# A hybrid attention and state-space block: the tables of W_out made earlier and kept in DRAM, and no elementwise sums on GpSimd behind the attention

## The chip, the cores and the metric

The kernel runs on one core of a Trainium2 chip. A core has TensorE (matmuls, PE in the profile; PEld is its weight load), VectorE (DVE), ScalarE (ACT), GpSimd (POOL) and SyncE (SP), which here only issues DMAs. Each engine works through its own list of instructions in order and waits at semaphores for the others; ScalarE's and GpSimd's lists can hold DMA issues too. The metric is the device time of one execution in microseconds: the median over runs.

## The reference

One layer on a sequence of 1024 tokens with 1024 features, float32. Cut to what matters:

```python
h = rms_norm(x, norm_gain)
q, k, v, z_a, u, z_s, g_a, g_s = split(h @ w_in)         # 4*512 + 2*512 + 2*1024 columns
y_a = (band_attention(q, k, v) * silu(z_a)) @ w_attn_out  # 8 heads of 64, chunks of 64, 9 chunks wide
y_s = gelu(s5_ssm(u))                                     # diagonal complex state space, 32 groups x 64 states
a, b = split(y_s @ w_glu + b_glu)
y_s = (a * sigmoid(b) * silu(z_s)) @ w_ssm_out
merged = sigmoid(g_a + bias_a) * y_a + sigmoid(g_s + bias_s) * y_s
out = rms_norm(x + merged @ w_out, final_gain)
```

The products have to keep float32 accuracy. The kernel splits each operand into a rounded part and the rest (`_hi` and `_lo`, type fp32r), and makes three matmuls of each product: hi x hi, lo x hi, hi x lo.

## The kernel before, in words

**Layout.** Features lie on the 128 partitions; a projection task makes 128 output features for all 1024 tokens, in two halves of 512 tokens, each accumulated in one of three PSUM banks (tag "mm"). A task is: load a block of weights (`w_raw`, 512 KB; `o_raw`, 256 KB, in the later stages), split it (`split_hi` on ScalarE, L100; `split_lo` on VectorE, L103), multiply (L106 to L108), evacuate each half. `Stream.run` loads and splits the weights of the next tasks while one is multiplied; w_hi, w_lo, o_hi and o_lo have two buffers each.

**Stages, in TensorE's order.** Norm and V; the projections of u, z and q, k with the state-space model beside them; the attention with q, k and the first five of eight g_a projections; the last g_a and the eight g_s projections (to 580 us: `ga_task`, `gs_task`, `sg` goes to DRAM as `sgs_dr`); the attention output (`a_task`, eight tasks, y_a times w_attn_out, evacuated by `mgd<-mm,mg`, L85); GLU (`glu_tasks`, eight, `zs<-zs,sg`); the SSM output (`so_task`, eight, `sg<-mm,sg` and `mgd<-mgd,sg`); and the final product with W_out.

**Beside the attention output** the state-space results are read back from DRAM in pieces of 512 bytes (`load_y`, tile `yr`) and split into `g_hi`, `g_lo`, the operands of GLU (`split_y_ssm`).

**The final product** uses Strassen's seven products instead of eight, on 2 x 2 blocks, for four blocks of 256 tokens. Its weight operands are seven tables for each of four row blocks j: B11, B21, B22 are blocks of W_out as they are, T1 to T4 are sums of them. Each table is a tile of hi and lo, 512 KB. `prepare_wo` loads two row blocks (`wo_raw`), lets GpSimd make the four sums (`t<-wo_raw`, `wo_raw<-wo_raw`, L85), and `keep` splits each table into its resident place `wb` (28 tiles, in places that `SPOTS` lists and that come free one after another). The loops over the attention output, GLU and SSM output call `next(tables)` to put a table's work between the tasks. The token side has its own sums: `derive` makes S1 to S4 (`s<-mgd`, on VectorE for the first token block and GpSimd for the others), `operand` splits them (`a`). `complete` adds up the squares and multiplies by the final gain (`x<-x,fg_b`, GpSimd).

**What sets the order.** The program is written task by task; a list scheduler with a model of the engines' and DMAs' times then orders the instructions of each engine by priority. Splits of weights have high priority. During the attention TensorE's order is as written. Tiles are reused as soon as their last reader is done, so a load into a used place waits for that reader, and what stands behind the load in its queue waits too. Before the change all loads of this part are issued by SyncE.

Of the kernel before, what the change touches and what calls it, by code (L numbers as in the profile page):

```python
# [44 lines left out]
def trunk_kernel(ctx: ExitStack, tc: tile.TileContext, x, x_t, ng, w_m, w_v, bias, a_re, a_im, log_dt,  # L45
# [38 lines left out]
    def tt(o, a, b, op, eng=None):  # L84
        (eng or vec).tensor_tensor(out=o, in0=a, in1=b, op=op)  # L85
# [1071 lines left out]
    def so_task(m, y):  # L1157
        sgs = []

        def load():  # L1160
            for half in range(2):
                sgs.append(half_tile())
                nc.sync.dma_start(out=sgs[half], in_=sgs_dr[m][:, cut(half)])

        loads.append(load)

        def before():

            for n in ([0, 1] if m == 0 else [m + 1] if m + 1 < KT else []):
                loads[n]()  # L1170

        def evac(half, ps):
            tt(sgs[half], ps, sgs[half], MUL)
            tt(merged(m, cut(half)), merged(m, cut(half)), sgs[half], ADD, pool if m < KT - 1 else vec)
        return o_task(w_so[m], y, evac, before, m == 0)

    zs = [None] * 4
# [1 line left out]
    def glu_tasks(m, y):  # L1179
        sgs = {}  # L1180

        def evac_b(half, ps):
            if half == 0:
                zs[m] = zp.tile([P, L], F32, tag="z", name="zs")
                nc.sync.dma_start(out=zs[m], in_=zs_dr[m])
            sgs[half] = half_tile()
            act.activation(out=sgs[half], in_=ps, func=AF.Sigmoid, bias=bg[:, 4 + m:5 + m])

        def evac_a(half, ps):
            sl = cut(half)  # L1190
            stt(sgs[half], ps, bg[:, m:m + 1], sgs[half], ADD, MUL)
            tt(zs[m][:, sl], zs[m][:, sl], sgs[half], MUL, pool if m < 3 else vec)

        return [o_task(w_glu[4 + m], y, evac_b), o_task(w_glu[m], y, evac_a)]

# [10 lines left out]
    def load_y(b):  # L1206
        yr = rows.tile([P, T8, NJ], F32, tag="yr", name="yr")
        nc.sync.dma_start(out=yr, in_=y_dr[b].rearrange("t p j -> p t j"))
        ygr.append(yr)

    gen = stream.run(ga[NGA:] + [gs_task(m) for m in range(KT)], a_all[:2])
    for _ in range(4 * KT):
        with tc.issue_after(last_turn[0]):
            next(gen)
    for b in range(2):
        load_y(b)
    for _ in gen:
        pass
    wp_cm.__exit__(None, None, None)
    h16_cm.__exit__(None, None, None)  # L1220
    wo_cm = tc.tile_pool(name="wo", reuse_waits="tile", side="right", bufs=14)
# [11 lines left out]
        yg[1].append(lo)  # L1233

    SPOTS = [(wo, "wb")] * 6 + [(qk_pools[n // 5], "blk") for n in range(10)] + [(wo, "wb")] * 8 + [(zp, "z")] * 4
    wb = {}
    raws = {}  # L1240

    def load_rows_wo(j):
        raws[j] = []
        for q in range(2):
            r = rows.tile([P, D], F32, tag="yr", name="wo_raw")
            nc.sync.dma_start(out=r, in_=w_out[(j + 4 * q) * P:(j + 4 * q + 1) * P, :])
            raws[j].append(r)

    def prepare_wo(j):

        def keep(name, src):
            p_, tag = SPOTS[len(wb)]
            t = p_.tile([P, 2, HALF], F32R, tag=tag, name="wb")
            split_hi(t[:, 0, :], src)
            split_lo(t[:, 1, :], src, t[:, 0, :])
            wb[name, j] = t

        def sum_tile():
            return rest.tile([P, HALF], F32, tag="t", name="t", bufs=1)

        b11, b12 = raws[j][0][:, cut(0)], raws[j][0][:, cut(1)]
        b21, b22 = raws[j][1][:, cut(0)], raws[j][1][:, cut(1)]
        t1 = sum_tile()
        tt(t1, b12, b11, SUB, pool)
        tt(b12, b22, b12, SUB, pool)
        keep("B11", b11)
        yield
        keep("T1", t1)
        t2 = sum_tile()
        tt(t2, b12, b11, ADD, pool)  # L1270
        yield
        keep("T3", b12)
        tt(b12, b21, t2, SUB, pool)
        yield
        keep("T2", t2)
        yield
        keep("B21", b21)
        yield
        keep("B22", b22)
        yield  # L1280
        keep("T4", b12)
        yield

    def all_wo():

        for j in range(4):
            load_rows_wo(j)
            yield
            yield
            for _ in prepare_wo(j):  # L1290
                yield

    tables = all_wo()

    for n, _ in enumerate(stream.run(a_all, glu[:2])):
        if n in (0, 1, 5, 6):
            split_y_ssm(len(yg[0]))
            if n < 2:
                load_y(n + 2)
        elif n > 6:  # L1300
            next(tables)
    for n, _ in enumerate(stream.run(glu, so_all[:2])):
        if n >= 3 and len(wb) < 16:
            next(tables)
    hs, ls = split_tiles(zs, vp, "v", "y", (3,))
    ys[0].extend(hs)
    ys[1].extend(ls)
# [13 lines left out]
        return t  # L1321

    for n, _ in enumerate(stream.run(so_all)):
        if n > 0:
            next(tables, None)
        if n == 2 * KT - 2:
            fin_op["A11"] = operand(block(0, "A11"), rows, "yr")
            s3 = rest.tile([P, HALF], F32, tag="t", name="s3", bufs=1).rearrange("p (k m) -> p k m", m=P)
            tt(s3, block(0, "A11"), block(0, "A21"), SUB, pool)
            fin_op["S3"] = operand(s3, rows, "yr")  # L1330
    assert len(wb) == 28
    rest_cm.__exit__(None, None, None)
# [24 lines left out]
    for n in range(KT // 2):  # L1357
# [5 lines left out]
            nc.sync.dma_start(out=xi[r], in_=x[tok[r], :])  # L1363
        ss = [fin.tile([P, 4], F32, tag=f"ss{r}", name="ss") for r in range(2)]
        blk = {b: block(n, b) for b in ("A11", "A12", "A21", "A22")}
        eng = vec if first else pool

        def derive(name, p, q, op):
            t = vp.tile([P, HALF], F32, tag="v", name="s")
            blk[name] = t.rearrange("p (k m) -> p k m", m=P)  # L1370
            tt(blk[name], blk[p], blk[q], op, eng)

        done = [0, 0]

        def complete(b, cs, end):

            r = b // 2
            col = slice((b % 2) * HALF + cs.start, (b % 2) * HALF + cs.stop)
            v = xi[r][:, col]
            sq = ps_v.tile([P, HALF], F32, tag="pv", name="sq")  # L1380
            act.activation(out=sq[:, :cs.stop - cs.start], in_=v, func=AF.Square, accum_out=ss[r][:, done[r]:done[r] + 1])
            if done[r] == 0:
                ts(ss[r][:, 3:4], ss[r][:, 0:1], 1.0 / D, MUL, 1e-6, ADD)
            else:
                stt(ss[r][:, 3:4], ss[r][:, done[r]:done[r] + 1], 1.0 / D, ss[r][:, 3:4], MUL, ADD)
            done[r] += 1
            cols[r].append(col)
            if not end:
                tt(v, v, fg_b[:, col], MUL, pool)
                return  # L1390
            inv = rsqrt(fin, ss[r][:, 3:4])
            for k, col in reversed(list(enumerate(cols[r]))):
                v = xi[r][:, col]
# [6 lines left out]
                (nc.scalar if k == 0 else nc.sync).dma_start(out=out[tok[r], col], in_=v)  # L1400
# [112 lines left out]
```

## Time and profile before

| | |
|---|---|
| median of three runs | 811.55 us (810.03 to 812.24) |
| the profiled execution | 809.46 us, span 807.7 us, clock 0.998 |
| TensorE, VectorE, ScalarE, GpSimd busy | 97%, 64%, 46%, 25% of the span |
| DMA | 76.22 MB, 94 GB/s in the mean |
| HBM read, written | 60.34 MB, 15.17 MB |

A row of the timeline has the start, the duration, the engine, the line, and the tile written <- the tiles read; in brackets stands how long the engine sat idle before and what ended that. A group's row has the number of instructions, their busy time and mean, and the idle time before them. TensorE's matmuls overlap: one starts every 0.23 us or so though each lasts 0.39, so lost time is read from their starts.

### The profile page before, as it was taken

What the parts mean: (1) busy time and instruction counts of PE and PEld (TensorE: products, weight loads), DVE (VectorE), ACT (ScalarE), POOL (GpSimd) and SP (SyncE); (2) the same over time, 40 slices, a digit from 0 to 9 for tenths busy, and PEclk for the clock granted to TensorE, in tenths of its full rate; (3) what the DMA queues carried; (4) which work ended last, traced back from release to release, by engine and by line L of the source; (5) the groups of instructions that cost most, each with busy time, mean ns of one, the idle gap of its engine ahead of it and who ended that gap; (6) DMA issues with size and microseconds to landing.
All of it is one profiled execution on the core that took longest, in us unless ns stands there. A gap on an engine that the chain in (4) does not pass through costs nothing. (4 is left out here: it accounts for less than half of the span.)

```text
span 807.7 us, 11038 instructions
## 1 busy us (share of the span) xinstructions
PE 786.7 (97%) x3882; PEld 650.8 (81%) x3882; DVE 515.6 (64%) x1324; ACT 371.5 (46%) x670; POOL 199.3 (25%) x220
## 2 busy tenths in 40 slices
PE   8999999999999999999999999999999999899996
PEld 6778888888887888888888888888867887788884
DVE  6899997978647788787445430111178338866684
ACT  5653455646436566666454572122253224322542
POOL 4560022020202323333122100000023223744431
PEclk9999999999999999999999999999999999999999
DMA  8703433233331011111000261231144114322332
GB/s 312 263 27 104 116 92 117 87 88 125 106 113 43 27 43 43 44 43 43 27 28 26 79 209 66 104 105 66 52 131 157 52 48 149 121 94 112 104 131 79
DMA packets 37063, 76.22 MB, mean 94 GB/s; under 512 B 5072, under 2 KB 14288, under 8 KB 37008
## 3 DMA queue, kind: packets, MB, share of 16 engines
q1 hardware_dynamic: 32512, 69.74, 25.6%
q0 software_dynamic: 1152, 2.36, 1.5%
q10 hardware_dynamic: 3344, 3.42, 1.3%
q8 instruction: 30, 0.49, 0.3%
q14 instruction: 25, 0.20, 0.1%
HBM read 60.34 MB, written 15.17 MB: 93 GB/s over the span
## 5 line engine op out<-in xcount | busy, mean ns | idle before, releaser
L106 PE MATMUL mm<-hT,w_hi 128*128 128x512 f32 x576 | 233.3, 405 | 0.0
L108 PE MATMUL mm<-hT,w_lo 128*128 128x512 f32 x576 | 226.1, 393 | 0.7 <-DVE w_lo L103 0.7
L107 PE MATMUL mm<-hT,w_hi 128*128 128x512 f32 x576 | 225.4, 391 | 0.0
L108 PEld LDWEIGHTS mm<-hT,w_lo 128*128 128x128 f32 x576 | 108.1, 188 | 24.6 <-DVE w_lo L103 1.1
L107 PEld LDWEIGHTS mm<-hT,w_hi 128*128 128x128 f32 x576 | 108.6, 189 | 16.6 <-issue 0.4
L106 PEld LDWEIGHTS mm<-hT,w_hi 128*128 128x128 f32 x576 | 108.4, 188 | 16.1 <-issue 0.2
L103 DVE TENSOR_TENSOR w_lo<-w_raw,w_hi 128x1024 fp32r<-128x1024 f32 x36 | 44.3, 1230 | 83.8 <-ACT w_hi L100 83.5
L939 POOL TENSOR_SCALAR p<-p,sm 128x640 f32<-128x640 f32 (+2 forms) x64 | 42.8, 671 | 111.3 <-DVE sm L938 80.8
L100 ACT ACTIVATE w_hi<-w_raw 128x1024 fp32r<-128x1024 f32 x36 | 38.1, 1058 | 68.8 <-PE mm L107 57.6
L937 ACT ACTIVATE p<-p,mx 128x640 f32<-128x640 f32 (+2 forms) x64 | 44.4, 694 | 33.3 <-DVE mx L89 16.5
L103 DVE TENSOR_TENSOR tl<-pt,th 128x512 fp32r<-128x512 f32 (+2 forms) x72 | 43.0, 600 | 24.5 <-ACT th L100 24.0
L100 ACT ACTIVATE th<-pt 128x512 fp32r<-128x512 f32 (+2 forms) x72 | 37.7, 523 | 44.5 <-PE pt L957 43.9
L930 DVE CUSTOM_DVE_ANT_0 p<-s,bias 128x320 f32<-128x320 f32 (+2 forms) x96 | 44.2, 485 | 17.1 <-PE s L929 16.7
L108 PE MATMUL mm<-y_hi,o_lo 128*128 128x512 f32 x128 | 50.2, 394 | 4.1 <-DVE o_lo L103 4.1
L106 PE MATMUL mm<-y_hi,o_hi 128*128 128x512 f32 x128 | 50.3, 394 | 1.9 <-ACT o_hi L100 1.1
L107 PE MATMUL mm<-y_lo,o_hi 128*128 128x512 f32 x128 | 49.8, 390 | 0.0
L85 POOL TENSOR_TENSOR t<-wo_raw 128x512 f32<-128x512 f32 x8 | 11.3, 1418 | 148.7 <-PE mm L108 129.9
L1427 PE MATMUL c<-wb,a 128*128 128x512 f32 (+1 forms) x116 | 44.8, 387 | 0.0
L1426 PE MATMUL c<-wb,a 128*128 128x512 f32 (+1 forms) x116 | 44.2, 387 | 0.5 <-DVE x L85 0.5
L1428 PE MATMUL c<-wb,a 128*128 128x512 f32 (+1 forms) x116 | 44.2, 385 | 0.0
L957 PE MATMUL pt<-ident,p 128*128 128x128 f32 x240 | 38.1, 273 | 0.0
L976 PE MATMUL pv<-tl,vt 128*128 128x256 f32 x144 | 36.2, 281 | 1.0 <-DVE tl L103 1.0
(230 smaller groups left out, 1533.4 us busy)
## 6 DMA issues: line engine op xcount, KB each, us to landing
w_raw<-in_w_m_dram SPq DMA_DIRECT2D x36, 512.0 KB, 3.5
x<-in_x_dram SPq DMA_DIRECT2D x16, 512.0 KB, 7.7
sgs_dr<-sg SPq DMA_DIRECT2D x16, 256.0 KB, 2.0
wo_raw<-in_w_out_dram SPq DMA_DIRECT2D x8, 512.0 KB, 3.5
sg<-sgs_dr SPq DMA_DIRECT2D x16, 256.0 KB, 2.9
xt<-in_x_t_dram SPq DMA_DIRECT2D x6, 512.0 KB, 9.6
bias<-in_bias_dram SPq DMA_DIRECT2D x8, 320.0 KB, 2.8
wv_raw<-in_w_v_dram SPq DMA_DIRECT2D x8, 256.0 KB, 5.6
```

Of the source, the lines that this page charges most:

```text
L100: act.activation(out=hi, in_=src, func=AF.Copy)
L103: (eng or vec).tensor_tensor(out=lo, in0=src, in1=hi.bitcast(F32), op=SUB)
L106: pe.matmul(ps, lh, rh, start=first, stop=False)
L107: pe.matmul(ps, lh, rl, start=False, stop=False)
L108: pe.matmul(ps, ll, rh, start=False, stop=last)
L930: vec.tensor_tensor_reduce(out=pr[:, c * cw:(c + 1) * cw], in0=ps, in1=bt[:, 640 - w + c * cw:640 - w + (c + 1) * cw], scale=1.0, scalar=- ...
L937: act.activation(out=pr[:, :w], in_=pr[:, :w], func=AF.Exp, bias=mx[:, 0:1], accum_out=sm)
L939: pool.tensor_scalar(out=pr[:, :w], in0=pr[:, :w], scalar1=sm, scalar2=1.0, op0=MUL, op1=MUL)
L957: last_turn[0] = pe.transpose(tp[:, n:n + P], probs[h, q][:, k * P:(k + 1) * P], ident).ins
L1426: pe.matmul(o, a[:, 0, k, :], h, start=new and k == 0, stop=False, skip_group_check=True)
L1427: pe.matmul(o, a[:, 0, k, :], l, start=False, stop=False, skip_group_check=True)
L1428: pe.matmul(o, a[:, 1, k, :], h, start=False, stop=k == 3, skip_group_check=True)
```

## The change

Four edits. (1) `make_tables` runs during the g_s projections, a step after every third matmul group: it loads the rows of W_out, makes the sums on VectorE, splits each table into one of the two free tiles of pool `blk1`, and stores it in DRAM (`wt_dr`, SyncE's queue). (2) `load_table` reads the 28 tables back into the same places as before, from ScalarE's queue, during the attention output, GLU and SSM output, in the order in which the final product uses them. (3) `load_y` of the first two blocks comes late in g_s instead of at its start, since its pool now holds `wo_raw`. (4) All sums and products that GpSimd made behind the attention are made by VectorE.

```diff
@@ so_task, glu_tasks
-            tt(merged(m, cut(half)), merged(m, cut(half)), sgs[half], ADD, pool if m < KT - 1 else vec)
+            tt(merged(m, cut(half)), merged(m, cut(half)), sgs[half], ADD)
-            tt(zs[m][:, sl], zs[m][:, sl], sgs[half], MUL, pool if m < 3 else vec)
+            tt(zs[m][:, sl], zs[m][:, sl], sgs[half], MUL)
@@ g_a, g_s
+    wt_dr = {(name, j): dr.tile([P, 2, HALF], F32, name=f"wt_{name}_{j}")
+             for name in ("B11", "B21", "B22", "T1", "T2", "T3", "T4") for j in range(4)}
+    def make_tables():
+        for j in range(4):
+            raws = []
+            for q in range(2):
+                r = rows.tile([P, D], F32, tag="yr", name="wo_raw")
+                nc.sync.dma_start(out=r, in_=w_out[(j + 4 * q) * P:(j + 4 * q + 1) * P, :])
+                raws.append(r)
+            yield
+            yield
+            def keep(name, src):
+                t = qk_pools[1].tile([P, 2, HALF], F32R, tag="blk", name="wt")
+                split_hi(t[:, 0, :], src)
+                split_lo(t[:, 1, :], src, t[:, 0, :])
+                nc.sync.dma_start(out=wt_dr[name, j], in_=t.bitcast(F32))
...
+            tt(t1, b12, b11, SUB)
+            tt(b12, b22, b12, SUB)
+            keep("T1", t1)
+            yield
+            keep("T3", b12)
...
-    for b in range(2):
-        load_y(b)
-    for _ in gen:
-        pass
+    for n, _ in enumerate(gen):
+        if n % 3 == 2:
+            next(tables, None)
+        if n in (3 * 36 + 4, 3 * 36 + 12):
+            load_y((n - 112) // 8)
@@ attention output, GLU, SSM output
-    def load_rows_wo(j):
-    def prepare_wo(j):
...
+    USE = ["B11", "T3", "B21", "T2", "T1", "B22", "T4"]
+    def load_table():
+        name, j = USE[len(wb) // 4], len(wb) % 4
+        p_, tag = SPOTS[len(wb)]
+        t = p_.tile([P, 2, HALF], F32R, tag=tag, name="wb")
+        nc.scalar.dma_start(out=t.bitcast(F32), in_=wt_dr[name, j])
+        wb[name, j] = t
     for n, _ in enumerate(stream.run(a_all, glu[:2])):
...
-        elif n > 6:
-            next(tables)
+        if n in (4, 7, 9, 11, 13, 15):
+            load_table()
     for n, _ in enumerate(stream.run(glu, so_all[:2])):
-        if n >= 3 and len(wb) < 16:
-            next(tables)
+        if n >= 2 and len(wb) < 16:
+            load_table()
     for n, _ in enumerate(stream.run(so_all)):
-        if n > 0:
-            next(tables, None)
+        if n > 1 and len(wb) < 28:
+            load_table()
@@ final product
-        eng = vec if first else pool
-            tt(blk[name], blk[p], blk[q], op, eng)
+            tt(blk[name], blk[p], blk[q], op)
-                tt(v, v, fg_b[:, col], MUL, pool)
+                tt(v, v, fg_b[:, col], MUL)
```

The scheduler puts the new work at these places. First ScalarE in the g_s projections: sg is the evacuation of a half (L1138), w_hi the split of the next weights. Before:

```order
L1138 ACTIVATE sg_5396<-mm_5371,gb_2612 128x512
L100 ACTIVATE w_hi_5461<-w_raw_5431 128x1024
L1138 ACTIVATE sg_5428<-mm_5403,gb_2612 128x512
L1138 ACTIVATE sg_5458<-mm_5433,gb_2612 128x512
L100 ACTIVATE w_hi_5523<-w_raw_5493 128x1024
```

and with the change, where wt is a table's buffer:

```order
L1138 ACTIVATE sg_5450<-mm_5417,gb_2612 128x512
L100 ACTIVATE wt_5457<-wo_raw_5348 128x512
L100 ACTIVATE wt_5471<-wo_raw_5348 128x512
L100 ACTIVATE w_hi_5540<-w_raw_5497 128x1024
L1138 ACTIVATE sg_5494<-mm_5461,gb_2612 128x512
L100 ACTIVATE wt_5515<-t_5512 128x512
L100 ACTIVATE wt_5528<-wo_raw_5484 128x512
L1138 ACTIVATE sg_5537<-mm_5499,gb_2612 128x512
L100 ACTIVATE wt_5551<-t_5532 128x512
L100 ACTIVATE wt_5565<-wo_raw_5484 128x512
L100 ACTIVATE w_hi_5623<-w_raw_5585 128x1024
```

Four table splits now stand between one w_hi and the next. Second, VectorE in the attention output, from the o_lo of the fourth task on. Before:

```order
L103 TENSOR_TENSOR o_lo_5961<-o_raw_5922,o_hi_5960 128x512
L103 TENSOR_TENSOR wb_6081<-wo_raw_6038,wb_6081 128x512
L103 TENSOR_TENSOR wb_6105<-t_6078,wb_6105 128x512
L85 TENSOR_TENSOR mgd_5872<-mm_5964,mg_4743 128x512
L103 TENSOR_TENSOR wb_6125<-wo_raw_6038,wb_6125 128x512
L85 TENSOR_TENSOR mgd_5872<-mm_5979,mg_4743 128x512
L103 TENSOR_TENSOR wb_6150<-t_6108,wb_6150 128x512
L103 TENSOR_TENSOR wb_6168<-wo_raw_6040,wb_6168 128x512
L103 TENSOR_TENSOR wb_6192<-wo_raw_6040,wb_6192 128x512
L103 TENSOR_TENSOR o_lo_6001<-o_raw_5958,o_hi_6000 128x512
```

and with the change, from the split of the last y_ssm block on:

```order
L103 TENSOR_TENSOR g_lo_6202<-yr_6100,g_hi_6201 128x1024
L85 TENSOR_TENSOR mgd_6052<-mm_6123,mg_4553 128x512
L103 TENSOR_TENSOR o_lo_6141<-o_raw_6102,o_hi_6140 128x512
L85 TENSOR_TENSOR mgd_6052<-mm_6144,mg_4743 128x512
L85 TENSOR_TENSOR mgd_6052<-mm_6161,mg_4743 128x512
L103 TENSOR_TENSOR o_lo_6183<-o_raw_6138,o_hi_6182 128x512
```

The six table splits (wb) between one o_lo and the next are gone. Third, VectorE in the SSM output. Before:

```order
L103 TENSOR_TENSOR wb_6896<-wo_raw_6740,wb_6896 128x512
L85 TENSOR_TENSOR sg_6629<-mm_6695,sg_6629 128x512
L103 TENSOR_TENSOR wb_6914<-wo_raw_6738,wb_6914 128x512
L103 TENSOR_TENSOR o_lo_6716<-o_raw_6667,o_hi_6715 128x512
L85 TENSOR_TENSOR sg_6673<-mm_6723,sg_6673 128x512
```

and with the change:

```order
L85 TENSOR_TENSOR sg_6758<-mm_6806,sg_6758 128x512
L85 TENSOR_TENSOR sg_6760<-mm_6823,sg_6760 128x512
L85 TENSOR_TENSOR mgd_6052<-mgd_6052,sg_6758 128x512
L85 TENSOR_TENSOR mgd_6052<-mgd_6052,sg_6760 128x512
L103 TENSOR_TENSOR o_lo_6843<-o_raw_6796,o_hi_6842 128x512
```

The two mgd sums that GpSimd made now stand ahead of the next o_lo, and the table splits are gone.

More of the change, by code (lines that the diff above doesn't have):

```diff
@@ L1209, in load_y, with sum_tile @@
         ygr.append(yr)
+    wt_dr = {(name, j): dr.tile([P, 2, HALF], F32, name=f"wt_{name}_{j}")
[14 more added lines that the diff above has]
+                nc.sync.dma_start(out=wt_dr[name, j], in_=t.bitcast(F32))
+            def sum_tile():
+                return rest.tile([P, HALF], F32, tag="t", name="t", bufs=1)
+            b11, b12 = raws[0][:, cut(0)], raws[0][:, cut(1)]
+            b21, b22 = raws[1][:, cut(0)], raws[1][:, cut(1)]
+            t1 = sum_tile()
+            tt(t1, b12, b11, SUB)
[3 more added lines that the diff above has]
+            keep("T3", b12)
+            t2 = sum_tile()
+            tt(t2, b12, b11, ADD)
+            yield
+            keep("T2", t2)
+            tt(b12, b21, t2, SUB)
+            yield
+            for name, src in (("T4", b12), ("B11", b11), ("B21", b21), ("B22", b22)):
+                keep(name, src)
+                yield
+    tables = make_tables()
     gen = stream.run(ga[NGA:] + [gs_task(m) for m in range(KT)], a_all[:2])
@@ L1238, in trunk_kernel @@
     SPOTS = [(wo, "wb")] * 6 + [(qk_pools[n // 5], "blk") for n in range(10)] + [(wo, "wb")] * 8 + [(zp, "z")] * 4
+    USE = ["B11", "T3", "B21", "T2", "T1", "B22", "T4"]
     wb = {}
-    raws = {}
-    def load_rows_wo(j):
[L1243 to L1247, printed above, removed]
-    def prepare_wo(j):
[L1251 to L1293, printed above, removed]
+    def load_table():
[4 more added lines that the diff above has]
+        wb[name, j] = t
     for n, _ in enumerate(stream.run(a_all, glu[:2])):
@@ L1328, in trunk_kernel @@
             s3 = rest.tile([P, HALF], F32, tag="t", name="s3", bufs=1).rearrange("p (k m) -> p k m", m=P)
-            tt(s3, block(0, "A11"), block(0, "A21"), SUB, pool)
+            tt(s3, block(0, "A11"), block(0, "A21"), SUB)
             fin_op["S3"] = operand(s3, rows, "yr")
```

## The prediction

> **What bounds the kernel now.** I read the page, then the busy time by stage, then what TensorE waited for, then the rows around those waits. TensorE is busy 97% of the span.
>
> ```profile
> PE 786.7 (97%) x3882; PEld 650.8 (81%) x3882; DVE 515.6 (64%) x1324; ACT 371.5 (46%) x670; POOL 199.3 (25%) x220
> ```
>
> Busy time is modelled, so I count the matmuls instead. In the g_s projections 24 of them run from 574.83 to 580.27 us, 0.2267 us each (two rows of TensorE's timeline; the second is the first row of the attention output):
>
> ```profile
> 574.83 0.39 PE L106 MATMUL mm<-hT,w_hi 128*128 128x512 f32 x1
> 580.27 0.39 PE L106 MATMUL mm<-y_hi,o_hi 128*128 128x512 f32 x1
> ```
>
> The windows are g_a/g_s, attention output, GLU, SSM output, final product; the first numbers are us, PE busy (count), PEld, DVE, ACT, POOL, then the granted clock, DMA share and GB/s:
>
> ```profile
> 480.00:580.00 100.00, 100.00 (x443) 82.81 (x442) 9.81 (x8) 21.90 (x29) 0.00 (x0) 1.00 0.22 77
> 580.27:629.51 49.24, 45.57 (x193) 35.41 (x192) 36.47 (x41) 21.60 (x27) 13.93 (x10) 1.00 0.40 129
> 629.51:674.31 44.80, 44.80 (x193) 35.91 (x192) 17.29 (x23) 15.74 (x25) 10.54 (x8) 1.00 0.21 60
> 674.31:721.22 46.91, 44.57 (x193) 35.68 (x192) 35.36 (x41) 11.77 (x21) 29.73 (x20) 1.00 0.39 129
> 721.22:799.91 78.69, 78.17 (x349) 63.48 (x347) 54.26 (x109) 32.44 (x72) 28.49 (x21) 1.00 0.27 101
> ```
>
> 192 matmuls need 43.5 us. The attention output takes 5.7 us more, GLU 1.3, SSM output 3.4. The final product has 336 full widths, 76.2 us, and takes 78.7 and the last 0.1: 2.6 more. So everything that can be won from 580 us on is 13.0 us, and 9.1 of it lies in two stages. There TensorE's waits are these (us in total, times, longest):
>
> ```profile
> PE mm L108 <- DVE o_lo L103: 4.1, 4, 1.5
> PE mm L106 <- ACT o_hi L100: 1.1, 1, 1.1
> PE mm L106 <- DVE mgd L85: 0.6, 1, 0.6
> PE mm L106 <- DVE sg L85: 0.2, 1, 0.2
> ```
>
> Seven waits, 6.0 us; with some 0.27 us hidden by the modelled ends at each, 7.9 of the 9.1. What made o_lo late, in rows of the timeline (start, us, engine): first VectorE in the attention output, then three engines in the SSM output:
>
> ```profile
> 604.95 1.28 DVE L103 TENSOR_TENSOR wb<-wo_raw,wb 128x512 fp32r<-128x512 f32 x2
> 606.15 0.68 DVE L103 TENSOR_TENSOR o_lo<-o_raw,o_hi 128x512 fp32r<-128x512 f32 x1
> ...
> 697.36 1.65 POOL L85 TENSOR_TENSOR mgd<-mgd,sg 128x512 f32<-128x512 f32 x1 [1.23 <-DVE sg L85]
> 697.81 1.75 DVE L103 TENSOR_TENSOR o_lo<-o_raw,o_hi 128x512 fp32r<-128x512 f32 x1
> 699.62 0.50 PE L108 MATMUL mm<-y_hi,o_lo 128*128 128x512 f32 x1 [1.48 <-DVE o_lo L103]
> ```
>
> Two causes: table splits (wb) stand ahead of o_lo on VectorE, and a split of two SBUF operands takes 1.75 us, not 0.68, while GpSimd adds. In the groups of 580 to 722 us the mean shows it, and mgd<-mm, which reads PSUM, does not have it:
>
> ```profile
> L103 DVE TENSOR_TENSOR wb<-wo_raw,wb 128x512 fp32r<-128x512 f32 x20 | 21.4, 1083 | 3.2 <-ACT wb L100 2.6
> L103 DVE TENSOR_TENSOR o_lo<-o_raw,o_hi 128x512 fp32r<-128x512 f32 x22 | 20.0, 909 | 7.3 <-ACT o_hi L100 7.3
> L85 DVE TENSOR_TENSOR mgd<-mm,mg 128x512 f32<-128x512 f32 x16 | 10.7, 681 | 4.2 <-PE mm L108 4.2
> ```
>
> **The change part by part.** *Attention and SSM output.* 28 splits (29 us of VectorE with their stretched durations) leave, and GpSimd is silent. VectorE gets 6 zs and 14 mgd sums here and the rest of these groups of GpSimd (580 to 808 us) in the final product:
>
> ```profile
> L85 POOL TENSOR_TENSOR mgd<-mgd,sg 128x512 f32<-128x512 f32 x14 | 21.4, 1540 | 7.5 <-DVE sg L85 7.5
> L85 POOL TENSOR_TENSOR x<-x,fg_b 128x512 f32<-128x512 f32 (+1 forms) x9 | 11.1, 1232 | 22.7 <-ACT sq L1381 19.3 <-DVE x L85 3.4
> L85 POOL TENSOR_TENSOR s<-mgd 128x512 f32<-128x512 f32 x7 | 10.6, 1513 | 23.0 <-DVE a L103 17.6 <-PE c L1428 5.3
> ```
>
> At 0.68 us an SSM task of 5.44 us then asks VectorE for two sg, two mgd and one o_lo: 3.4 us. So I leave 0.4 us of the SSM output's 3.4 (its scattered part): gain 3.0, bounds 2 and 3.4. In the attention output one wait stays. The fourth task starts at 580.3 + 3 x 5.44 = 596.6 and its o_lo is needed at 597.0, but it stands behind the last y_ssm split (VectorE's timeline; the last row is an issue of a DMA by ScalarE, from the final product):
>
> ```profile
> 594.24 2.03 DVE L103 TENSOR_TENSOR g_lo<-yr,g_hi 128x1024 fp32r<-128x1024 f32 x1 [0.22 <-ACT g_hi L100]
> 596.78 0.68 DVE L103 TENSOR_TENSOR o_lo<-o_raw,o_hi 128x512 fp32r<-128x512 f32 x1
> 753.49 0.39 ACTq L1400 DMA_DIRECT2D out_dram<-x  x1
> ```
>
> That is 0.4 us late at today's times. The new order puts table loads of 512 KB beside the last two loads of yr, 1.5 us each at the 355 GB/s worked out below, and two issues of 0.39 us on ScalarE ahead of this o_hi. Bounds 0.4 and 0.4 + 2 x 1.5 = 3.4; I take 1.4, nearer to today's row, because the issues run while VectorE still splits yr. With 0.4 scattered, gain 5.7 - 1.8 = 3.9. GLU had no named wait: 0.
>
> *The tables in g_s.* 28 ScalarE and 28 VectorE splits, 16 sums, 28 stores and 8 loads enter a stage where VectorE is busy 10% and ScalarE 22%: 17.6 us more on ScalarE, 30 on VectorE; the 92 us from 488 hold that. What can cost is waiting: in the new order ScalarE has four tables between one w_hi and the next, each waits for one of two buffers, and a buffer is free when its store has landed. Behind it stand sg and w_hi, and TensorE waits for those. The rows: two w_hi on ScalarE's timeline, the page's group of w_lo, a split of a table on ScalarE today, and DMA issues with KB and us to landing.
>
> ```profile
> 504.08 1.06 ACT L100 ACTIVATE w_hi<-w_raw 128x1024 fp32r<-128x1024 f32 x1 [4.52 <-PE mm L107]
> 514.97 1.06 ACT L100 ACTIVATE w_hi<-w_raw 128x1024 fp32r<-128x1024 f32 x1 [4.52 <-PE mm L107]
> ...
> L103 DVE TENSOR_TENSOR w_lo<-w_raw,w_hi 128x1024 fp32r<-128x1024 f32 x36 | 44.3, 1230 | 83.8 <-ACT w_hi L100 83.5
> ...
> 598.64 0.63 ACT L100 ACTIVATE wb<-t 128x512 fp32r<-128x512 f32 x1 [1.06 <-POOL t L85]
> ...
> w_raw<-in_w_m_dram SPq DMA_DIRECT2D x36, 512.0 KB, 3.5
> x<-in_x_dram SPq DMA_DIRECT2D x16, 512.0 KB, 7.7
> ...
> zs_dr<-zst SPq DMA_DIRECT2D x4, 512.0 KB, 2.9
> ```
>
> A w_hi is needed one task, 10.9 us, after it is made; less 1.06 and VectorE's 1.23 for w_lo, 8.6 us of slack. A table's cycle is 0.63 for the first split, 0.68 for the second, 0.39 for the issue and the landing of a 512 KB store: 2.9 in zs_dr's row, so 4.6 us, 2.3 per table with two buffers. The order spreads the 28 over 7.4 tasks of 10.9 us, 80 us, 2.9 each. With c = (1.7 + landing) / 2 the landing may grow to 4.7 us before 28 x (c - 2.9) eats the 8.6. Will it? The stage moves 14.7 MB of stores, 3.1 of w_out rows, 3.7 of w_raw, 3.9 of sg in 80 us: 318 GB/s. Three windows of today, with DMA share and GB/s at the end:
>
> ```profile
> 500.00:520.00 20.00, 20.00 (x90) 16.53 (x89) 2.45 (x2) 3.96 (x5) 0.00 (x0) 1.00 0.29 103
> 560.00:580.00 20.00, 20.00 (x90) 16.57 (x89) 0.80 (x1) 2.20 (x4) 0.00 (x0) 1.00 0.13 52
> 466.00:474.00 8.00, 8.00 (x37) 6.60 (x36) 0.63 (x1) 7.96 (x15) 1.20 (x1) 1.00 0.93 288
> ```
>
> 103 GB/s at share 0.29 is 355 GB/s for a full share, the stores of sg alone 52 / 0.13 = 400, the small pieces of yr 288 / 0.93 = 310. So the engines are 80 to 103% full. Cost: none up to 8.6 us of lag, 42 us with a landing like x's 7.7 (28 x (4.7 - 2.9) - 8.6; the run's first loads). I take 0, near the stores' own row.
>
> The Trainium skill, "HBM Reference", section Latency, speaks against that: an access takes 0.2 us on average and 2 us at high load. By it a store here would land some 1.8 us later, 4.7, just at the edge; the sum would lose 0 to 2 us (an estimate from that page). No run here shows a loaded store yet.
>
> *Final product and end.* VectorE takes over 12 derived sums and 9 products with fg_b, 8.3 + 5.8 = 14.1 us at 0.68 each: at most 54.3 + 14.1 = 68.4 of 78.7 us, 87%, less what GpSimd stretches now. TensorE has no wait there but 0.5 us at the end. Cost 0.2, bounds 0 and 14.1. At the end, GpSimd's and VectorE's timeline:
>
> ```profile
> 799.13 0.73 POOL L85 TENSOR_TENSOR x<-x,fg_b 128x256 f32<-128x256 f32 x1 [2.48 <-ACT sq L1381]
> ...
> 799.18 0.70 DVE L94 SCALAR_TENSOR_TENSOR rs_u<-rs_r,ss 128x1 f32<-128x1 f32 x1
> 800.97 0.42 DVE L85 TENSOR_TENSOR x<-c,x 128x256 f32<-128x256 f32 x1
> ```
>
> rs_u takes 0.70 under the GpSimd product and the last sum waits behind; the order after puts fg_b's half width (0.4) before rs_u (0.2) and the sum ahead of the long product. Gain 0.4, bounds 0 and 0.7.
>
> **Sum.** 3.9 + 3.0 + 0.4 - 0.2 = 7.1 us. The profiled execution took 809.46 us in all (span 807.7); so 802.4. The median of the runs shown, 811.55, is 2.1 above it: 804.4, say 804.5.
>
> **Rivals.** *The tables bind g_s* (the other side). Place: ScalarE's wait for a table buffer, with w_hi and sg behind it; it decides from a landing of 4.7 us. At 5.0 us 28 x 0.45 - 8.6 = 4.0 us are lost, 808.5; at 6.0, with c = 3.85, 18 us, 822. For it: 80 to 103% full engines. Against: 400 GB/s of stores, and lag up to 8.6 us costs nothing. *Only one stage is cleared:* yr lands 3.4 us late and the attention output keeps its waits, or o_lo is late in the SSM output for another reason than GpSimd: 807.5. *VectorE becomes the bound of the final product:* its queue is in order, and a derived sum (0.68) now stands ahead of the split that a product waits for. It decides when the lead of the splits falls under 0.7 us of a product's 2.72; at worst all 14.1 us show, 818.5. Against it stand 13% of free VectorE at the least. *The change does nothing:* if TensorE's lateness came from ScalarE's o_hi alone (1.1 of 6.0 us), 810.5; the rows at 606 and 699 speak against.
>
> **How the numbers follow.** Forecast 802 to 806.5: 0.70. One stage: 0.10. Tables bind: 0.06 with a small loss (807 to 810), 0.07 slower. Final product: 0.05, nothing: 0.02. A measurement of this kernel can tell 0.3%, 2.4 us: faster is below 809.1, slower above 814. Faster 0.70 + 0.10 + 0.02 = 0.82, of which I give 0.02 away for run-to-run spread; same 0.04 + 0.02 + 0.01 + that = 0.09; slower 0.11. The range 801.5 to 809.5 leaves out the slow rivals and half of the rest.
>
> **What would show it.** Right: o_lo gone from TensorE's waits after 600 us; o_lo at 0.68 us mean; 49.24 and 46.91 us become about 45.3 and 43.9; no wait of TensorE in 480 to 580, DMA share there about 0.9; VectorE under 68 us in the final product. Wrong: waits for w_lo or sg in g_s, table stores landing after 5 us, or waits for a in the final product.

## The result, and the profile after

The changed kernel took 799.86 us in the median of four runs (799.41 to 801.95), beside 811.66 for the kernel before, also of four: a ratio of 0.986, 95% interval 0.984 to 0.989. Timed again in the experiments below, 800.20 beside 810.61, 0.988 (0.986 to 0.989). Forecast were 804.5 us, 801.5 to 809.5: the direction was right, the gain 10.4 to 11.8 us where 7.1 stood in the sum, and the time came out below the range.

First the page's busy times; the profiled execution took 801.95 us:

```profile
PE 786.2 (98%) x3882; PEld 654.3 (82%) x3882; DVE 533.2 (67%) x1382; ACT 371.4 (46%) x670; POOL 115.6 (14%) x162
```

Then the busy time by stage with the columns known from before: g_a/g_s, attention output, GLU, SSM output, final product:

```profile
480.00:580.00 100.00, 100.00 (x442) 82.78 (x442) 38.06 (x50) 38.56 (x59) 0.00 (x0) 1.00 0.79 285
582.73:626.55 43.82, 43.82 (x193) 35.88 (x192) 22.13 (x26) 13.02 (x12) 0.00 (x0) 1.00 0.67 228
626.55:671.36 44.81, 44.81 (x194) 35.91 (x193) 19.49 (x27) 13.63 (x21) 0.00 (x0) 1.00 0.36 113
671.36:714.89 43.53, 43.53 (x193) 36.03 (x192) 29.68 (x46) 6.81 (x11) 0.00 (x0) 1.00 0.61 217
714.89:793.19 78.30, 77.78 (x348) 63.50 (x347) 59.56 (x130) 32.53 (x71) 0.00 (x0) 1.00 0.28 101
```

The attention output went from 49.24 to 43.82 us, the SSM output from 46.91 to 43.53, and both are now within 0.3 us of the 43.5 that their 192 matmuls need. The tables' way through DRAM raises the DMA traffic from 76.22 to 105.58 MB. Of the seven waits of TensorE none is left; from 440 us to the end its waits are one line:

```profile
PE c L1423 <- DVE x L85: 0.5, 1, 0.5
```

The splits and sums on VectorE in 580 to 720 us have the duration that was assumed for them, o_lo 0.69 us and not 0.91:

```profile
L103 DVE TENSOR_TENSOR o_lo<-o_raw,o_hi 128x512 fp32r<-128x512 f32 x22 | 15.1, 686 | 11.4 <-ACT o_hi L100 11.4
L85 DVE TENSOR_TENSOR mgd<-mgd,sg 128x512 f32<-128x512 f32 x16 | 10.9, 688 | 0.3
```

In g_s, where the tables went, VectorE and ScalarE are busy four tenths of the time, the DMA engines 79%, and TensorE is never held up. How near it came shows on ScalarE's timeline in two w_hi, seven tasks apart, and on the page in the stores of tables (DMA issues, KB, median us to landing):

```profile
484.78 1.06 ACT L100 ACTIVATE w_hi<-w_raw 128x1024 fp32r<-128x1024 f32 x1 [3.86 <-PE mm L107]
564.91 1.04 ACT L100 ACTIVATE w_hi<-w_raw 128x1024 fp32r<-128x1024 f32 x1
```

```profile
wt_T<-wt SPq DMA_DIRECT2D x16, 512.0 KB, 3.4
...
wt_B<-wt SPq DMA_DIRECT2D x12, 512.0 KB, 4.3
```

Seven tasks of 10.88 us are 76.2; the two w_hi lie 80.1 apart. So in this profile the last one was 4.0 us behind its time, out of the 8.6 that it had. That is the largest lag in any profile; in the second profile of the same kernel the two lie 76.5 apart, a lag of 0.4:

```profile
482.98 1.06 ACT L100 ACTIVATE w_hi<-w_raw 128x1024 fp32r<-128x1024 f32 x1 [3.86 <-PE mm L107]
559.51 1.04 ACT L100 ACTIVATE w_hi<-w_raw 128x1024 fp32r<-128x1024 f32 x1
```

In kernels 2 and 4 to 7 of the experiments, which make the tables in the same way, the lag is 0.4 to 1.2 us.

### The profile page after: what moved, and what is told of

Its sections match the earlier page's. It is cut to its first block, busy times and chain, and to the rows that moved or that the text cites. A ratio compares the mean times of both kernels' runs of the same rounds, so it can differ in the third digit from the quotient of the medians.

```text
span 800.2 us, 11133 instructions
## 1 busy us (share of the span) xinstructions
PE 786.2 (98%) x3882; PEld 654.3 (82%) x3882; DVE 533.2 (67%) x1382; ACT 371.4 (46%) x670; POOL 115.6 (14%) x162
## 2 busy tenths in 40 slices
DMA packets 45127, 105.58 MB, mean 132 GB/s; under 512 B 5968, under 2 KB 15184, under 8 KB 45072
## 4 chain that ended last, share of the span: by engine, by line
PE 89%; DVE 6%; ACT 1%; issue 1%; DMA 1%; POOL 0%; DVEq 0%; ACTq 0%
PE mm L108 22%; PE mm L106 22%; PE mm L107 22%; PE c L1423 3%; PE c L1424 3%; PE c L1425 3%; PE pt L957 2%; PE pv L976 2%; PE s L928 1%; PE pv L975 1%; DVE p L930 1%; PE s L929 1%; DVE tl L103 1%; PE pt L456 1%; PE b L482 1%
## 5 line engine op out<-in xcount | busy, mean ns | idle before, releaser
L100 ACT ACTIVATE o_hi<-o_raw 128x512 fp32r<-128x512 f32 x24 | 15.1, 632 | 70.1 <-PE mm L107 55.5
```

Of the source, the lines that this page charges most:

```text
L100: act.activation(out=hi, in_=src, func=AF.Copy)
```

## Experiments

Every profile can be cut at the same five places. The stages of the changed kernel repeat within 0.05 us, those of the kernel before within 0.2 but for its attention output, 0.6, so such a row tells more than a time of the whole. The kernels have the numbers of their labels. "Start" is the first matmul of the projections with hT, "to attention output" what lies between it and the first matmul of that stage, "tail" what follows the last matmul's start; all in us, from TensorE's timeline and the span (given to 0.1 us, so the tail is good to 0.05). Kernels 3 to 7 and 9 were executed once each, so their times hold the start of that one execution, and only their stages are compared.

| kernel | start | to attention output | attention output | GLU | SSM output | final product | tail |
|---|---|---|---|---|---|---|---|
| before | 56.03 | 524.24 | 49.24 | 44.80 | 46.91 | 78.69 | 7.79 |
| before, again | 58.25 | 524.39 | 48.60 | 44.79 | 46.74 | 78.60 | 7.73 |
| changed | 58.45 | 524.28 | 43.82 | 44.81 | 43.53 | 78.30 | 7.01 |
| changed, again | 56.54 | 524.39 | 43.87 | 44.80 | 43.54 | 78.30 | 6.96 |
| 1 no GpSimd sums, tables in place | 58.03 | 524.38 | 47.14 | 44.94 | 44.95 | 78.61 | 7.05 |
| 2 tables early, GpSimd sums | 56.28 | 524.35 | 43.77 | 44.81 | 43.54 | 79.53 | 7.72 |
| 3 every table stored twice | 55.42 | 524.23 | 43.56 | 52.54 | 43.54 | 78.30 | 7.21 |
| 4 a spare buffer tile, unused | 57.83 | 524.50 | 43.79 | 44.80 | 43.54 | 78.30 | 6.94 |
| 5 four loads beside yr | 55.48 | 524.29 | 45.72 | 44.80 | 43.54 | 78.30 | 6.97 |
| 6 final gain on GpSimd | 58.28 | 524.33 | 43.76 | 44.80 | 43.54 | 78.29 | 7.70 |
| 7 derived blocks on GpSimd | 56.12 | 524.38 | 43.77 | 44.80 | 43.54 | 78.28 | 7.01 |
| 9 one table buffer | 56.29 | 524.38 | 50.29 | 44.80 | 43.54 | 78.30 | 7.00 |

**Both kernels once more.** The question was where the part of the gain lies that the stages don't show.

> The kernel before, unchanged, profiled once more. If the granted clock at the start of an execution varies from one to the next whatever the kernel, the first 20 us differ again from the first profile (where the clock was 1.00 from 8 to 20 us) while the stages from the attention output on repeat: 49.2, 44.8, 46.9, 78.7 us within 0.3 each, tail 7.8. If instead the dip belongs to the change, the first 20 us are as in the first profile.

> The changed kernel, unchanged, profiled and timed once more. Theory: the change is worth the sum of its stages, 5.4 + 3.4 + 0.4 + 0.8 = 10.0 us, and nothing before 580 us; the rest of the 11.8 us between the medians is the spread of executions. Then the difference here is 10 to 11 us, a ratio of 0.986 to 0.988, the four stages repeat at 43.8, 44.8, 43.5 and 78.3 us, and the first 440 us take the same as in the kernel before wherever the granted clock does. Rival: about 1.8 us more are won ahead of 580 us by the change itself; then the difference is 11.5 to 12 us and the attention output starts some 1.8 us earlier than in the kernel before at the same clock.

Of the kernel before, the granted clock of the start in its second profile, and of the changed one the first projection matmul in its first profile:

```profile
8.00:12.00 4.00, 2.94 (x8) 1.77 (x9) 2.41 (x3) 1.96 (x4) 2.91 (x3) 0.72 0.92 314
12.00:16.00 4.00, 4.00 (x16) 3.23 (x15) 4.00 (x6) 3.06 (x6) 1.16 (x2) 0.85 1.02 386
```

```profile
58.45 0.63 PE L106 MATMUL mm<-hT,w_hi 128*128 128x512 f32 x2
```

The start differs from execution to execution, 55.4 to 58.5 us in twelve profiles, whatever the kernel; from there to the attention output all take 524.2 to 524.5 us. The tables cost g_s nothing that could be measured. The clock is part of the spread at most: kernel 1 had 1.00 throughout and started at 58.03. Taking means of two profiles each, the change is worth 48.92 - 43.85 + 46.83 - 43.54 + 78.65 - 78.30 + 7.76 - 6.99 = 9.5 us behind 580 us. The 10.4 of the second timing is 0.9 above that and the 11.8 of the first 2.3, both within what the start varies by. So the rival, 1.8 us won ahead of 580, has nothing for it: from the start to the attention output both kernels take 524.2 to 524.4 us, and each has one long and one short start.

**Each half alone (kernels 1 and 2).** Kernel 1 is the kernel before with these sums on VectorE; the tables stay in place. Kernel 2 is the changed kernel with them back on GpSimd.

```diff
 # kernel 1, against the kernel before (the same for all of GpSimd's sums from mgd, zs and w_out on)
-        tt(t1, b12, b11, SUB, pool)
+        tt(t1, b12, b11, SUB)
-        eng = vec if first else pool
+        eng = vec
 # kernel 2, against the changed kernel (and zs, S3, derive and fg_b in the same way)
-            tt(merged(m, cut(half)), merged(m, cut(half)), sgs[half], ADD)
+            tt(merged(m, cut(half)), merged(m, cut(half)), sgs[half], ADD, pool if m < KT - 1 else vec)
```

> Of the change only one half: every sum of GpSimd behind the attention runs on VectorE, and the tables are still made in place during the attention output, GLU and SSM output. Theory (two causes: table splits stand ahead of o_lo on VectorE, and splits of two SBUF operands are stretched while GpSimd adds): o_lo and the table splits all take 0.68 to 0.70 us, yet in the attention output splits and 4 sums per row group of w_out still stand ahead of o_lo, so that stage goes from 49.2 to 46 to 48 us, the SSM output from 46.9 to 43.6 to 45, final product and tail as in the changed kernel (78.3 and 7.0); total 803 to 806. Rival A (the stretch is the whole cause): 43.8 and 43.6 us, total 800 to 801, and the tables in DRAM are needless. Rival B (VectorE's place in the queue is the whole cause): attention output 49 us or more, SSM output 46 to 47; total 809 to 812.

> Of the change only the other half: the tables are made during g_s and kept in DRAM, but the sums of mgd, zs, S3, the derived blocks and the products with the final gain run on GpSimd as in the kernel before. Theory (two causes): attention output 43.8 us as in the changed kernel, since GpSimd has nothing there; in the SSM output o_lo is stretched again (a mean of about 0.9 over the run) with nothing of the tables ahead of it, so 44.5 to 46 us; final product 78.7 and tail 7.8 as before; total 2.2 to 3.7 us above the changed kernel, 802 to 804. Rival A (the stretch is the whole cause): the attention output keeps some of its waits and the SSM output is 46.9; total 804 to 808. Rival B (place in the queue is the whole cause): 43.8 and 43.5, total as the changed kernel or up to 1.2 above (final product and tail).

Kernel 1: 804.69 us, ratio 0.993 (0.991 to 0.995). Its attention output, SSM output, and what TensorE waited for from 560 us on:

```profile
582.41:629.55 47.14, 45.25 (x193) 35.49 (x192) 35.10 (x49) 21.17 (x27) 0.00 (x0) 1.00 0.39 129
...
674.49:719.44 44.95, 44.30 (x194) 35.73 (x192) 37.97 (x62) 11.82 (x21) 0.00 (x0) 1.00 0.40 135
```

```profile
PE mm L106 <- DVE mgd L85: 1.1, 3, 0.6
PE mm L108 <- DVE o_lo L103: 0.6, 1, 0.6
PE mm L106 <- ACT wb L100: 0.6, 1, 0.6
```

All splits there take 0.68 us, and yet the attention output takes 3.3 us more than in the changed kernel and the SSM output 1.4, for a table's sums and splits still stand ahead of o_lo and mgd. Here the sum t waits for a load of W_out, and o_lo, whose o_hi was done at 596.61, stands behind it:

```profile
599.04 0.69 DVE L85 TENSOR_TENSOR t<-wo_raw 128x512 f32<-128x512 f32 x1 [0.29 <-DMA wo_raw<-in_w_out_dram]
599.65 0.68 DVE L103 TENSOR_TENSOR o_lo<-o_raw,o_hi 128x512 fp32r<-128x512 f32 x1
...
600.39 0.50 PE L108 MATMUL mm<-y_hi,o_lo 128*128 128x512 f32 x1 [0.65 <-DVE o_lo L103]
```

Kernel 2: 801.66 us, ratio 0.989 (0.988 to 0.991). Its SSM output and final product by stage, the o_lo group of that SSM output and the same group in the kernel before, and one row of VectorE's timeline in kernel 2:

```profile
669.21:712.75 43.54, 43.54 (x194) 36.03 (x193) 22.15 (x31) 6.82 (x11) 20.96 (x15) 1.00 0.60 216
712.75:792.28 79.53, 78.29 (x348) 63.37 (x347) 53.78 (x109) 32.28 (x71) 29.40 (x21) 1.00 0.27 100
```

```profile
L103 DVE TENSOR_TENSOR o_lo<-o_raw,o_hi 128x512 fp32r<-128x512 f32 x7 | 6.6, 936 | 2.7 <-ACT o_hi L100 2.7
L103 DVE TENSOR_TENSOR o_lo<-o_raw,o_hi 128x512 fp32r<-128x512 f32 x7 | 9.0, 1281 | 0.0
```

```profile
692.95 1.79 DVE L103 TENSOR_TENSOR o_lo<-o_raw,o_hi 128x512 fp32r<-128x512 f32 x1
```

GpSimd is busy 21 us of this stage. A single o_lo is stretched as far as before (1.79 us), but fewer of them are: two of seven, with a mean of 0.94 us, where the kernel before has five of seven and 1.28. TensorE doesn't wait once. This I had not expected: without tables in VectorE's list a stretched split is in time. So the tables' place alone is enough to make both stages late (kernel 1); in the SSM output the stretch added to it while the tables were there, and what is left of the stretch without them costs nothing. In the attention output kernel 2 says nothing of the stretch, for GpSimd is idle there once the tables' sums are gone. Kernel 2 also has the loads from ScalarE's queue and the later load_y, which weren't taken apart. That GpSimd is silent bought nothing in the SSM output; what it bought in kernel 2's terms is 79.53 - 78.30 in the final product and 7.72 - 6.99 in the tail.

**The final product and the tail (kernels 6 and 7).** Each gives one kind of product back to GpSimd in the changed kernel.

```diff
 # kernel 6
-                tt(v, v, fg_b[:, col], MUL)
+                tt(v, v, fg_b[:, col], MUL, pool)
 # kernel 7, and S3 the same
-            tt(blk[name], blk[p], blk[q], op)
+            tt(blk[name], blk[p], blk[q], op, vec if first else pool)
```

> The changed kernel, but the products with the final gain (fg_b, 9 of them, the last one of half width at the very end) run on GpSimd as before. Theory: the tail behind the last matmul goes from 7.0 back to 7.7 or 7.8 us (rs_u at 0.70 instead of 0.2 under the GpSimd product, and the last sum behind it), the final product stays at 78.3: total 0.7 to 0.8 us above the changed kernel at the same start. Rival: the final product grows too, to 79.5 us as with all of GpSimd's sums, because the stretched splits of a come from these products; total 2 us above.

> The changed kernel, but the derived blocks of the final product (8 of the 12 sums there, and S3) run on GpSimd as before; the products with the final gain stay on VectorE. With all of GpSimd's sums back, the final product took 79.5 us and the tail 7.7; with only the products back, 78.3 and 7.7. Theory (the derived sums make GpSimd stretch VectorE's splits of a, and a sum that frees a PSUM bank stands behind such a split): final product 79.0 to 79.6 us, tail 7.0; total 0.7 to 1.3 us above the changed kernel at the same start. Rival (it takes both together): 78.3 and 7.0, no difference.

They took 802.50 and 799.64 us. The tail is the gain product's alone, 0.7 us. Three rows each of VectorE's timeline at the end, kernel 6 and then the changed kernel:

```profile
792.26 0.70 DVE L94 SCALAR_TENSOR_TENSOR rs_u<-rs_r,ss 128x1 f32<-128x1 f32 x1
...
793.38 0.75 DVE L94 SCALAR_TENSOR_TENSOR x<-x,rs_r,fg_b 128x512 f32<-128x512 f32 x1
794.05 0.42 DVE L85 TENSOR_TENSOR x<-c,x 128x256 f32<-128x256 f32 x1
```

```profile
792.78 0.21 DVE L94 SCALAR_TENSOR_TENSOR rs_u<-rs_r,ss 128x1 f32<-128x1 f32 x1
...
793.51 0.42 DVE L85 TENSOR_TENSOR x<-c,x 128x256 f32<-128x256 f32 x1
793.85 0.74 DVE L94 SCALAR_TENSOR_TENSOR x<-x,rs_r,fg_b 128x512 f32<-128x512 f32 x1
```

The last matmul starts at 793.00 and at 793.19, so the last sum follows it by 1.05 us in kernel 6 and by 0.32 in the changed one. Both parts of the forecast's step are there, the short rs_u (0.5) and the sum ahead of the long product. For the final product my theory fell: neither kind alone costs anything (78.29 and 78.28); kernel 2, which has both and the mgd and zs sums too, loses 1.2. Why the kernel before, with the same sums on GpSimd, lost only 0.35 there stays open; the order of its 348 matmuls, as far as their lines tell it, is that of kernel 2.

**What the landing of the stores does (kernels 3, 4 and 9).**

```diff
 # kernel 3, in keep()
                 nc.sync.dma_start(out=wt_dr[name, j], in_=t.bitcast(F32))
+                nc.sync.dma_start(out=wt_two[name, j], in_=t.bitcast(F32))
 # kernel 4, in keep()
+                qk_pools[1].tile([P, 2, HALF], F32R, tag="blk", name="wt_idle")
 # kernel 9, ahead of g_s, and behind it
+    held = qk_pools[1].tile([P, 2, HALF], F32R, tag="blk", name="held")
+    pool.memset(held[:, 0, 0:1].bitcast(F32), 0.0)
...
+    nc.gpsimd.dma_start(out=held[:, 1, :].bitcast(F32), in_=sgs_dr[6][:, cut(1)])
```

> The changed kernel, but every table is stored to a second place in DRAM too (28 more stores of 512 KB in g_s; nothing reads them). The stage then moves 14.7 x 2 + 3.1 + 3.7 + 3.9 = 40.1 MB in 80 us, and a table's buffer is free only when both stores have landed. Theory (the stores' landing sets ScalarE's table cycle, the slack of 8.6 us covers it): at 355 GB/s 40.1 MB need 113 us, so a lag of 33 us less 8.6 is lost as waits of TensorE for w_hi, w_lo or sg in 500 to 590 us: 24 us, total 824; bounds 812 (400 GB/s) and 841 (310 GB/s). Rival (stores are hidden whatever their number, the transfers run beside everything): total 800, DMA share up, no wait of TensorE.

> The changed kernel with one table buffer in g_s instead of two (every second buffer is given to a tile that is never used). A table's cycle is then the whole 0.63 + 0.68 + 0.39 + landing: with a landing of 2.9 (zs_dr in the kernel before) to 4.3 us (wt_B in the changed kernel) 4.6 to 6.0 us for each of 28 tables, 129 to 168 us where 80 + 8.6 are free. Theory: 40 to 79 us lost, total 840 to 880, TensorE waits for w_hi, w_lo or sg. Rival (tables never hold ScalarE's queue up, since VectorE and ScalarE have enough room): total 800 to 801.

> The changed kernel, but one of the two table buffers of g_s is held by a tile that is written ahead of g_s and again by a small load behind its next-to-last task, so that tables really take turns in one buffer. A cycle is 0.63 + 0.68 + 0.39 + landing of 2.9 to 4.3 = 4.6 to 6.0 us, 129 to 168 us for 28 from 488 us on, so the last table is split at 617 to 656 us. Theory (the planned order sees the wait, keeps w_hi and sg in time and pushes the tables behind g_s, as it did with the doubled stores, where the last was split at 608 us and GLU lost 9): no wait of TensorE in 500 to 580; the y_ssm splits stand behind the tables, GLU waits for g_hi and g_lo, total 815 to 860. Rival (the order stays, ScalarE's queue makes w_hi late): waits for w_hi, w_lo or sg in 500 to 590, 840 to 880. Rival (landing is hidden): total 800 to 802.

They took 806.60, 801.55 and 806.38 us. Kernel 4 tells nothing: a tile that nothing touches takes no buffer, tables still took turns in two, and its row in the table is that of the changed kernel. Kernel 3 by stage (g_s, attention output, GLU), and TensorE's waits from 480 us on:

```profile
488.00:570.00 82.00, 82.00 (x364) 67.91 (x363) 27.84 (x36) 29.21 (x45) 0.00 (x0) 1.00 0.91 345
579.65:623.21 43.56, 43.56 (x193) 36.03 (x192) 22.93 (x33) 12.70 (x16) 0.00 (x0) 1.00 0.96 350
623.21:675.75 52.54, 47.68 (x193) 37.12 (x192) 24.36 (x30) 17.32 (x23) 0.00 (x0) 0.94 0.54 185
```

```profile
PE mm L106 <- ACT g_hi L100: 4.1, 1, 4.1
PE mm L107 <- DVE g_lo L103: 0.8, 1, 0.8
```

Twice the stores, DMA engines 91 to 96% full, and still nothing is lost in g_s: w_hi comes every 10.88 us exactly, up to 557.87. The scheduler knows of the second store; it had put fewer tables between two w_hi, and the last tables fell behind g_s, the last of them split at 607.94. The yr splits come behind those, and GLU waited 4.9 us for them and then ran on at a granted clock of 0.70 in 630 to 640 us (0.94 in the mean of the stage): 7.7 us in all. In kernel 9 the attention output paid; its waits of TensorE from 480 us on, and the rows around the longest:

```profile
PE mm L106 <- DVE mgd L85: 2.4, 1, 2.4
PE mm L108 <- DVE o_lo L103: 1.3, 1, 1.3
PE mm L106 <- ACT o_hi L100: 0.7, 1, 0.7
```

```profile
621.30 1.92 DVE L103 TENSOR_TENSOR g_lo<-yr,g_hi 128x1024 fp32r<-128x1024 f32 x1 [3.37 <-ACT g_hi L100]
623.15 0.68 DVE L85 TENSOR_TENSOR mgd<-mm,mg 128x512 f32<-128x512 f32 x1
...
623.97 0.76 PE L106 MATMUL mm<-y_hi,o_hi 128*128 128x512 f32 x1 [2.40 <-DVE mgd L85]
```

All three waits are for an instruction behind a split of yr: this mgd and the o_lo at 610.10 behind a g_lo, the o_hi at 608.11 behind a g_hi. The loads of yr, whose pool also holds wo_raw, start at 598.65 us here and at 566.13 in the changed kernel. With 4.4 us of waits, and a granted clock of 0.83 in 620 to 630 us, the stage lost 50.29 - 43.85 = 6.4 us. The theory was right that g_s would not pay and that the yr splits would come late; it was wrong in place (GLU) and size (15 us or more). The cycle in one buffer was as reckoned, 17 steps from 488.98 to 575.99 us or 5.1 each, but the second buffer came free at 577.9, and the last table was split at 604 us and not at 617 or later.

**The price of a load beside yr (kernel 5).** In the changed kernel the table loads stand in ScalarE's queue; here four go by SyncE's, between the last two loads of yr.

```diff
             if n < 2:
                 load_y(n + 2)
+            if n == 0:
+                for _ in range(4):
+                    with tc.issue_after(last_y[0].ins):
+                        load_table(nc.sync)
...
-        if n in (4, 7, 9, 11, 13, 15):
+        if n in (13, 15):
             load_table()
```

> The changed kernel, but four table loads of 512 KB are issued by SP right behind the third yr load, ahead of the fourth (in the changed kernel ScalarE issues them, and one lies beside these two loads). It measures the term that was put at 1.5 us per load. Theory of the prediction: four loads delay the fourth yr by up to 6 us, ScalarE begins its split 15 to 18 us after the attention output's first matmul instead of 11.5. TensorE loses little by that here, for the planned order now puts the fourth task's o_lo ahead of that yr's split on VectorE: total 800 to 802. Rival (loads beside yr cost yr nothing): the split begins at 11.5 to 12 us.

It took 800.89 us. ScalarE's timeline in kernel 5 and in the changed kernel, the third and fourth yr each:

```profile
588.76 2.06 ACT L100 ACTIVATE g_hi<-yr 128x1024 fp32r<-128x1024 f32 x1 [2.90 <-DMA yr<-y_dr]
...
598.74 2.04 ACT L100 ACTIVATE g_hi<-yr 128x1024 fp32r<-128x1024 f32 x1 [7.40 <-DMA yr<-y_dr]
```

```profile
590.77 0.33 ACTq L1290 DMA_DIRECT2D wb<-wt_T  x1
591.70 2.06 ACT L100 ACTIVATE g_hi<-yr 128x1024 fp32r<-128x1024 f32 x1 [2.88 <-DMA yr<-y_dr]
594.24 2.08 ACT L100 ACTIVATE g_hi<-yr 128x1024 fp32r<-128x1024 f32 x1 [0.49 <-DMA yr<-y_dr]
594.25 1.51 ACTq L1290 DMA_DIRECT2D wb<-wt_B  x3
```

Counted from the stage's first matmul (579.77 and 582.73) the fourth yr's split began at 18.97 instead of 11.51 us, 7.5 later. 0.9 of that is a later issue; the rest is the landing, 10.6 us after the issue instead of 4.0, for four loads ahead of it in its own queue and one of ScalarE's: 1.3 to 1.6 us each. TensorE lost 1.9 us by it, where I had expected little. So the price was right. What was wrong is that it would be paid: in the changed kernel the loads from 594.25 us on stand in ScalarE's list behind the split that waits for yr, and the only one beside that yr was issued at 590.77, 0.6 us behind it; the fourth yr landed in 4.0 us like the third.

## Why the prediction was right or wrong

- **The attention output, gain 3.9 forecast, 5.1 measured (5.4 in the first pair of profiles): the step that failed.** Of 5.7 us I kept 1.8: 0.4 scattered and 1.4 at the fourth task's o_lo. Both parts of the 1.4 were wrong. The 0.4 "late at today's times" was reckoned from a task start of 596.6; TensorE's own rows of the kernel before show that the task began at 597.01 and that o_lo, ready at 597.46, was just in time for the third matmul (in the changed kernel the same task loses under 0.2 us):

```profile
597.01 0.47 PE L106 MATMUL mm<-y_hi,o_hi 128*128 128x512 f32 x1
597.31 0.40 PE L107 MATMUL mm<-y_lo,o_hi 128*128 128x512 f32 x1
597.55 0.46 PE L108 MATMUL mm<-y_hi,o_lo 128*128 128x512 f32 x1
```

  The 1.0 for two loads beside yr had about the right price per load (kernel 5) and the wrong count, for none stood ahead of yr: yr's splits began 8.97 and 11.51 us into the stage, beside 9.06 and 11.87 before. The 0.4 of scattered time was about right: 43.85 is 0.3 above the 43.5 of the matmuls.
- **The SSM output, 3.0 forecast, 3.3 measured.** The 0.4 kept as scattered went with the waits: 43.54. The reason was half right. Kernel 2 shows that moving the tables away is enough, kernel 1 that silencing GpSimd alone wins 1.9 of it. The two causes were right as causes of a late o_lo, but they don't add: in these kernels the stretch cost only where tables stood in the list.
- **GLU 0:** 0 within 0.02. Its 1.3 us above the 43.5 stand in every kernel (44.8 to 44.9, but for kernel 3), with matmuls 44.80 / 192 = 0.2333 us apart instead of 0.2267 and no wait; why is open.
- **g_s 0:** right. The last w_hi was 4.0 us late in the first profile and 0.4 to 1.2 in the six others with this g_s, of the 8.6 that it had. The Trainium skill, "HBM Reference", section Latency, gives 0.2 us for an access on average and 2 us at high load, from which the prediction estimated a store that lands 1.8 us later. The trace gives 3.4 and 4.3 us beside 2.9, so 0.5 to 1.4 more, at a DMA share of 0.79 in 480 to 580 us and 0.88 in 500 to 560; it goes the way the Trainium skill says, by less. The rival that tables bind g_s was wrong in its mechanism too: in kernels 3 and 9 the surplus was moved behind g_s and paid there, 7.7 and 6.4 us, where 24 were expected of kernel 3 and 15 to 60 of kernel 9.
- **The final product, -0.2 forecast, +0.35 measured.** VectorE was busy 59.6 us, under the 68.4 bound, and the lead of the splits held. The rival of VectorE as bound has nothing for it.
- **The tail, 0.4 forecast, 0.7 to 0.8 measured.** I counted the shorter rs_u and left out most of the 0.75 us product that the last sum no longer stands behind.
- **The base, the other step that failed.** The terms fell short by 9.5 - 7.1 = 2.4 us: 1.2 in the attention output, 0.3 in the SSM output, 0.5 in the final product, 0.4 in the tail. The rest of the miss, 2.2 us, is the step from 802.4 to 804.5. With every term as measured the forecast would have been 804.5 - 2.4 = 802.1, inside the range; from the profiled 809.46 the same terms give 800.0, beside 799.9 measured. The median of three lay 2.1 above the profiled execution, and that of the eleven later runs, 810.61, only 1.2; for the changed kernel it fell the other way, and the median lies 2.1 below the profiled time. In the profiles the start is what varies by so much (before 56.03 and 58.25, changed 58.45 and 56.54); that it also set the times of the executions without a profile is likely but not shown. That the two draws went apart was bad luck; that a spread of this size had no place in the sum was the error.
- **The signs named in advance** came: no o_lo in the waits after 600 us, o_lo at 0.69, no wait in 480 to 580. The stages fell further than the 45.3 and 43.9 named, and the DMA share in 480 to 580 us was 0.79, not 0.9.
- The Trainium skill, "SBUF — State Buffer", section Who interferes with whom, says that a VectorE instruction with two SBUF inputs contends with a GpSimd instruction that reads SBUF, and that one with at most one SBUF input, outside the modes that use both ports, doesn't. The runs agree: in the SSM output the mean of o_lo is 0.68 us in kernel 1 and 0.94 in kernel 2, while sg<-mm,sg, with one input in PSUM, stays at 0.69 in both.

## What to carry to other kernels

Count a wait from the waiting engine's own rows, not from a task length times a number; the rows were there. When two causes make an instruction late, ask whether either one alone does: here the work ahead of it in the list did, and what was left of the stretch cost nothing once the list had room. A median of three runs is a base with a spread of its own: where executions differ by 2 us, a forecast of 7 us needs that in its range. And where a scheduler plans the order with the cost in sight, an extra cost may be paid not where it arises but where the displaced work lands (kernels 3 and 9), so look for the price in the next stages too.

## What the runs showed of the hardware that I had not expected

- The first 56 us of an execution vary by 3.1 us (twelve profiles), in steps that look like two groups, 55.4 to 56.5 and 57.8 to 58.5, while the 524 us that follow repeat within 0.3. In 8 to 16 us the granted clock went as low as 0.5 in some executions and stayed at 1.00 in others; the group isn't told by it alone, and its cause stays open.
- A 128x1 instruction of VectorE took 0.70 us instead of 0.21 while GpSimd worked on a 128x256 product of 0.73 us: next to GpSimd a small instruction can cost as much as a large one.
- The DMA engines ran at shares of 0.91 to 0.96 in two stretches of 82 and 44 us, at 345 to 350 GB/s (kernel 3), and the stores of 512 KB, issued in pairs, landed in 4.9 (wt_T) and 6.3 us (wt_B) in the median.
- A wait of TensorE cost more than its length. Behind the waits of kernel 3 its matmuls started 0.43 us apart up to 636 us, where 0.23 is usual, at a granted clock of 0.70 in 630 to 640; behind the last of kernel 9 they came 0.43 apart too, at 0.83 in 620 to 630. The stages lost 7.7 us with 4.9 of waits, and 6.4 with 4.4 (some 0.3 us of each wait is hidden by the modelled ends of the matmuls).
